# Modulation of a two-layer generator block: from column products on VectorE with sums on TensorE to row products on GpSimd, ScalarE and VectorE

## The chip, the cores and the metric

The kernel runs on one core of a Trainium2 chip, which has five engines with a queue each: TensorE (PE in the profile, PEld its weight loads), VectorE (DVE), ScalarE (ACT), GpSimd (POOL) and SyncE (SP), which issues most DMAs. Each engine takes its queue in order. The metric is the device time of one execution in microseconds (us), as the median of several runs.

## The reference

Two trunk layers over 256 context tokens and 1024 latent tokens, 1024 channels, all in 32-bit floats. What the change touches is the modulation: six vectors of 1024 numbers for each layer and each of two conditioning rows (`c` for the latents, `c_ctx` for the context).

```python
for layer in range(DEPTH):            # 2
    mod_l = (silu(c)     @ w_ada[layer] + b_ada[layer])      # w_ada: (2, 1024, 6144)
    mod_c = (silu(c_ctx) @ w_ada[layer] + b_ada[layer])
    sh1, sc1, g1, sh2, sc2, g2 = split(mod, 6)               # for _l and _c
    p = split_proj((rmsnorm(x) * (1 + sc1) + sh1) @ w_in[layer])
    x = x + g1 * mixer_out(four_scans(p), p, g_heads[layer], w_out[layer])
    x = x + g2 * square(relu((rmsnorm(x) * (1 + sc2) + sh2) @ w_ff1[layer])) @ w_ff2[layer]
return rmsnorm(x) * g_final
```

## The kernel before

Channels lie on the 128 partitions and tokens along the free dimension (NT = 1280 of both kinds). Large products are three matmuls each (`mm3`, lines 291 to 295), since every operand is split into a high and a low half; `whalf` (line 275) loads a weight tile of 128x512, makes its high half on ACT (line 281) and its low half on DVE (line 282).

For each layer `build` runs the norm and the projection of values (`mix_open`), then the four head groups (`mixers`), the output projection (`outproj`) and the channel sub-layer (`mlp`). In `mixers` two streams are interleaved: the scans (`mix_vec`, `mix_ml`, `mix_rt`, much of it on DVE and ACT) and dense projections that fill PE (`Fill`). In `mlp` 16 pairs of hidden tiles follow each other: 6 blocks of 24 matmuls, whose results ACT and DVE square and split (lines 502 to 505), then 24 blocks of 6 matmuls, which DVE adds into the residual (line 525, an "evacuation" below).

The modulation `mod` has 48 columns of 128 for each layer, in three parts r of 16 columns. Part 0 of layer 0 is made ahead on PE (`ada_unit`, `ada_finish`). The other five parts are made beside other work by the generator `ada_part` (line 391). It goes over a group of W columns: for each k of 8 it loads w_ada of 128 input channels by W columns (line 402), multiplies every partition by its conditioning number, and adds to an accumulator A on DVE (line 406 for k = 0, line 408 after), one accumulator for each conditioning row. Then PE sums A over the partitions with a vector of ones, 128 columns at a time (line 413, one output column each), and DVE adds the bias (line 419) and, for the scales, 1 (line 421).

- Parts 1 and 2 of layer 0 run in `mixers` of layer 0: W = 256, four weight buffers, both rows from one load, 128 loads of 128 KB. `Fill.step` takes a step of the generator (one load with its products) at three of five of its own steps (line 175); what is left runs at the end (line 1500).
- The three parts of layer 1 run in `mlp` of layer 0: W = 512, four weight buffers, 96 loads of 256 KB, four steps after each hidden tile (`filler`, line 1611). Parts 1 and 2 need the latents' row alone.

The order of the instructions on each engine is worked out when the program is built, by readiness of operands and buffers, and not by the order of the source alone; at run time it is fixed. All loads named here are issued by SP.

Of the kernel before, what the change touches and what calls it, by code (L numbers as in the profile page):

```python
# [6 lines left out]
F32 = mybir.dt.float32  # L7
# [190 lines left out]
class K:  # L198
    def __init__(self, ctx, tc, io):
# [16 lines left out]
        self.d_a = dp.tile([2, 4, NC], F32, name="d_a")  # L216

# [105 lines left out]

    def params2(self, tmp):
# [66 lines left out]
    def ada_part(self, l, r, toks, wring, tmp, acc, banks, W):  # L391


        nc = self.nc
        one = self.m64[:, 1:2]
        nt, nb = len(toks), W // 128
        for q in range(2048 // W):
            g, h = divmod(q * W, 512)
            A = [b(W) for b in acc[:nt]]
            for k in range(NK):  # L400
                w = wring.next()(W)
                nc.sync.dma_start(w, self.io["w_ada"][l, r, k, :, g, h:h + W])
                for i, j in enumerate(toks):
                    c = self.cc[:, k, j:j + 1]
                    if k == 0:
                        nc.vector.tensor_scalar(A[i], w, c, None, op0=ALU.mult)
                    else:
                        nc.vector.scalar_tensor_tensor(A[i], w, c, A[i], op0=ALU.mult, op1=ALU.add)
                yield
            ps = self.bank(banks().next())  # L410
            for i in range(nt):
                for cb in range(nb):
                    nc.tensor.matmul(ps[:, 2 * cb + i:2 * cb + i + 1], lhsT=A[i][:, 128 * cb:128 * cb + 128], rhs=one,  # L413
                                     start=True, stop=True)
            o = 16 * r + nb * q
            mo = self.mod[:, l, o:o + nb, toks[0]:toks[0] + nt]
            bb = self.bada[:, l, o:o + nb].unsqueeze(2).to_broadcast([128, nb, nt])
            v = ps[:, 0:2 * nb].rearrange("p (c j) -> p c j", j=2)[:, :, 0:nt]
            nc.vector.tensor_tensor(mo, v, bb, op=ALU.add)
            if (r == 0 and g >= 2) or (r == 2 and g < 2):  # L420
                nc.vector.tensor_scalar(mo, mo, 1.0, None, op0=ALU.add)
            yield
# [997 lines left out]
    def mixers(self, l, ada):  # L1420
# [36 lines left out]
        if l == 0:  # L1457
            fill.also = ada([ao.sub(256 * i, 256) for i in range(6)], lambda: self.dbanks)
# [112 lines left out]
def build(ctx, tc, io):  # L1571
# [16 lines left out]
    b.params2(b.tmps.next())  # L1588
    for l in range(2):
# [148 lines left out]
```

## Time and profile before

| | |
|---|---|
| median of 3 runs | 3310.36 us (3309.62 to 3310.97) |
| profiled execution | 3300.05 us |
| its span, first to last instruction | 3298.2 us |
| mean granted TensorE clock | 0.992 |
| busy: PE, PEld, DVE, ACT, POOL | 97%, 80%, 64%, 39%, 0% |
| chain that ended last | PE 88%, DVE 5%, DMA 3%, ACT 3% |
| mixers of layer 0 | about 220 to 770 us |
| channel sub-layer of layer 0 | about 930 to 1840 us |

Busy time is the union of an engine's instructions; matmuls are pipelined, so a busy PE is one that always has one under way. The chain is followed back from the last instruction to what released it at each step. A wait is told by the waiting engine and line, and what released it.

### The profile page before, as it was taken

Reading aid. Unit: us, or ns where it says so; the run is one execution under the profiler, and the core shown is the slowest. Engines: PE = TensorE matmul, PEld = TensorE weight load, DVE = VectorE, ACT = ScalarE, POOL = GpSimd, SP = SyncE. Lnnn points to the kernel's source line nnn. Section 1 sums busy time; section 2 is a strip of 40 time slices with the busy share of each in tenths; the row PEclk is TensorE's granted clock in tenths of the full one; section 3 lists DMA queues with packets and bytes.
Section 4 is the critical chain, followed back from the end, with each engine's and each line's share of the span. In section 5 each row is a group of like instructions: output and inputs, shape, how many; then the busy total and the mean of one; then the engine's idle time right before and its main releaser. Section 6 shows DMA issues by size and latency. Waiting matters only on the chain.

```text
span 3298.2 us, 52930 instructions
## 1 busy us (share of the span) xinstructions
PE 3215.6 (97%) x20936; PEld 2640.0 (80%) x20936; DVE 2121.8 (64%) x4218; ACT 1286.1 (39%) x2665; POOL 10.8 (0%) x41
## 2 busy tenths in 40 slices
PE   7998899999999999999999999999999999999998
PEld 4786688877888888888888678788778888888887
DVE  4778887787666656555655586866756555554546
ACT  4665565445322122121212565765445322222222
POOL 0000000000000000000000000000000000000000
PEclk9999899999999999999999999999999999999999
DMA  5113444434322222222211222333315111111111
GB/s 206 61 50 127 122 133 148 121 101 146 103 80 71 83 65 80 69 64 64 77 39 34 76 66 77 110 114 109 103 58 163 53 50 46 51 51 46 51 48 65
DMA packets 175010, 278.85 MB, mean 85 GB/s; under 512 B 21097, under 2 KB 66825, under 8 KB 174505
## 3 DMA queue, kind: packets, MB, share of 16 engines
q1 hardware_dynamic: 173464, 273.66, 26.5%
q8 instruction: 164, 2.69, 0.3%
q10 hardware_dynamic: 1296, 1.81, 0.2%
q14 instruction: 86, 0.70, 0.1%
HBM read 229.75 MB, written 45.64 MB: 83 GB/s over the span
## 4 chain that ended last, share of the span: by engine, by line
PE 88%; DVE 5%; DMA 3%; ACT 3%; issue 1%; SPq 0%; DVEq 0%; ACTq 0%
PE psum L293 23%; PE psum L294 23%; PE psum L295 23%; PE psum L830 2%; PE psum L600 2%; PE psum L631 2%; PE psum L633 2%; PE psum L632 1%; PE psum L817 1%; PE psum L833 1%; PE psum L1018 1%; PE psum L705 1%; PE psum L1357 1%; PE psum L413 1%; DVE px L990 1%
## 5 line engine op out<-in xcount | busy, mean ns | idle before, releaser
L525 DVE SCALAR_TENSOR_TENSOR x<-psum,st,x 128x512 f32<-128x512 f32 (+1 forms) x648 | 441.3, 690 | 213.2 <-PE psum L295 212.3
L281 ACT ACTIVATE pc<-st 128x512 fp32r<-128x512 f32 x256 | 161.2, 632 | 847.5 <-PE psum L294 808.7
L294 PE MATMUL psum<-pc,pc 128*128 128x512 f32 (+1 forms) x1296 | 475.9, 367 | 0.0
L293 PE MATMUL psum<-pc,pc 128*128 128x512 f32 (+1 forms) x1296 | 475.8, 367 | 0.0
L295 PE MATMUL psum<-pc,pc 128*128 128x512 f32 (+1 forms) x1296 | 473.8, 366 | 0.0
L293 PE MATMUL psum<-Hhi,pc 128*128 128x512 f32 (+1 forms) x1280 | 471.9, 369 | 1.7 <-ACT pc L281 1.5
L294 PE MATMUL psum<-Hlo,pc 128*128 128x512 f32 (+1 forms) x1280 | 471.9, 369 | 0.1
L295 PE MATMUL psum<-Hhi,pc 128*128 128x512 f32 (+1 forms) x1280 | 470.5, 368 | 0.0
L293 PE MATMUL psum<-Hhi,pw 128*128 128x512 f32 (+1 forms) x1192 | 451.0, 379 | 5.7 <-ACT pw L281 2.5
L295 PE MATMUL psum<-Hhi,pw 128*128 128x512 f32 (+1 forms) x1192 | 445.2, 374 | 0.0
L294 PE MATMUL psum<-Hlo,pw 128*128 128x512 f32 (+1 forms) x1192 | 444.8, 373 | 0.0
L504 DVE TENSOR_TENSOR st<-st 128x256 f32<-128x256 f32 (+1 forms) x160 | 101.8, 637 | 301.8 <-ACT pc L503 300.7
L293 PEld LDWEIGHTS psum<-pc,pc 128*128 128x128 f32 x1296 | 244.4, 189 | 43.8 <-DVE x L525 1.3
L295 PEld LDWEIGHTS psum<-pc,pc 128*128 128x128 f32 x1296 | 244.0, 188 | 43.0 <-issue 2.7
L294 PEld LDWEIGHTS psum<-pc,pc 128*128 128x128 f32 x1296 | 244.5, 189 | 41.3 <-issue 2.1
L293 PEld LDWEIGHTS psum<-Hhi,pc 128*128 128x128 f32 x1280 | 241.2, 189 | 43.5 <-ACT pc L281 2.4
L294 PEld LDWEIGHTS psum<-Hlo,pc 128*128 128x128 f32 x1280 | 241.3, 189 | 40.9 <-DVE Hlo L481 0.5
L295 PEld LDWEIGHTS psum<-Hhi,pc 128*128 128x128 f32 x1280 | 241.1, 188 | 40.9 <-DVE pc L282 0.6
L293 PEld LDWEIGHTS psum<-Hhi,pw 128*128 128x128 f32 x1192 | 226.7, 190 | 51.4 <-issue 10.1
L282 DVE TENSOR_TENSOR pc<-st,pc 128x512 fp32r<-128x512 f32 x256 | 175.5, 690 | 137.9 <-ACT pc L281 117.3
L295 PEld LDWEIGHTS psum<-Hhi,pw 128*128 128x128 f32 x1192 | 226.2, 190 | 37.6 <-issue 2.1
L294 PEld LDWEIGHTS psum<-Hlo,pw 128*128 128x128 f32 x1192 | 226.8, 190 | 36.2 <-issue 2.2
(398 smaller groups left out, 4950.4 us busy)
## 6 DMA issues: line engine op xcount, KB each, us to landing
st<-w_ff SPq DMA_DIRECT2D x256, 256.0 KB
st<-w_inT SPq DMA_DIRECT2D x96, 256.0 KB
ph<-w_ada SPq DMA_DIRECT2D x128, 128.0 KB
st<-w_out SPq DMA_DIRECT2D x50, 256.0 KB
pc<-w_ada SPq DMA_DIRECT2D x48, 256.0 KB
st<-w_ada SPq DMA_DIRECT2D x48, 256.0 KB
d_z<-st SPq DMA_DIRECT2D x40, 256.0 KB
ps<-w_ada SPq DMA_DIRECT2D x32, 256.0 KB
```

What stands on the lines that cost most here:

```text
L281: nc.scalar.activation(hi, raw, AF.Copy)
L282: (eng or nc.vector).tensor_tensor(lo, raw, F(hi), op=ALU.subtract)
L293: t.matmul(out, lhsT=w[0], rhs=m[0], start=first, stop=False)
L294: t.matmul(out, lhsT=w[0], rhs=m[1], start=False, stop=False)
L295: t.matmul(out, lhsT=w[1], rhs=m[0], start=False, stop=last)
L413: nc.tensor.matmul(ps[:, 2 * cb + i:2 * cb + i + 1], lhsT=A[i][:, 128 * cb:128 * cb + 128], rhs=one, start=True, stop=True)
L504: nc.vector.tensor_tensor(r, r, r, op=ALU.mult)
L525: nc.vector.scalar_tensor_tensor(x, ps, self.mod[:, l, 40 + o, j:j + 1], x, op0=ALU.mult, op1=ALU.add)
L600: t.matmul(ps[:, 0:304], lhsT=h[a], rhs=u[b], start=(k + i == 0), stop=(k == NK - 1 and i == 2))
L631: t.matmul(ps[:, e, :], lhsT=h[0], rhs=u[0], start=(k == 0), stop=False)
L633: t.matmul(ps[:, e, :], lhsT=h[1], rhs=u[0], start=False, stop=(k == NK - 1))
L830: nc.tensor.matmul(o, lhsT=ST[r0:r0 + kd, c, d, :], rhs=qd[d](c)[r0:r0 + kd, :], start=(j == 0), stop=False, tile_position=(r0, 0))
```

## The change

The loads now hold rows of the transposed weights: 128 output columns on the partitions and 512 of the 1024 input channels along the free dimension (`w_adaR`, laid out on the host). The conditioning row must then lie along the free dimension, the same on each partition: `cond_rows` transposes the 16 conditioning columns on PE once, writes them to DRAM (`d_c`), and `ada_rows` fetches half a row at a time to all partitions. One step multiplies a load by the row and sums it along the free dimension into one column of a scratch, which lies in that part of `mod` that belongs to the other layer. In layer 0's mixers GpSimd multiplies and ScalarE sums, by a copy that also gives out its sum (two weight buffers and one for the row, 256 KB a load, 128 loads, since each conditioning row now has its own loads). In layer 0's `mlp`, for layer 1, one VectorE instruction does both (five weight buffers and one for the row, 128 loads of 256 KB); a step there is two loads, and three steps follow a hidden tile. The two halves are added and the bias and the 1 follow on VectorE. PE has no part in it.

```diff
+    def cond_rows(self, tmp):
...
+        T = self.bank(self.banks.next())[0:16, 0:128]
+        a, b = tmp.sub(0, 16)(16), tmp.sub(16, 128)(128)
+        nc.vector.tensor_copy(a.rearrange("p (j k) -> p k j", k=NK), self.cc[:, :, 0:2])
+        nc.tensor.transpose(T, a, self.ident)
+        nc.vector.tensor_copy(b[0:16], T)
+        nc.gpsimd.dma_start(self.d_c.rearrange("j k p -> (j k) p"), b[0:16])
...
-    def ada_part(self, l, r, toks, wring, tmp, acc, banks, W):
...
+    def ada_rows(self, l, r, toks, wring, cs, queue, several=1):
...
+        S = self.mod[:, 1 - l, 0:16, :]
+        for j in toks:
+            for h in range(2):
+                c = cs.next()(512)
+                queue.dma_start(c.rearrange("p (k q) -> p k q", q=128), self.d_c[j:j + 1, 4 * h:4 * h + 4, :].to_broadcast([128, 4, 128]))
+                for o in range(16):
+                    w = wring.next()(512)
+                    queue.dma_start(w, self.io["w_adaR"][l, r, o, :, 512 * h:512 * h + 512])
+                    if l == 0:
+                        nc.gpsimd.tensor_tensor(w, w, c, op=ALU.mult)
+                        nc.scalar.activation(w, w, AF.Copy, accum_out=S[:, o:o + 1, h])
                     else:
+                        nc.vector.scalar_tensor_tensor(w, w, 1.0, c, op0=ALU.mult, op1=ALU.mult, accum_out=S[:, o:o + 1, h])
+                    if o % several == several - 1:
+                        yield
+            mo = self.mod[:, l, 16 * r:16 * r + 16, j]
+            nc.vector.tensor_tensor(mo, S[:, :, 0], S[:, :, 1], op=ALU.add)
+            nc.vector.tensor_tensor(mo, mo, self.bada[:, l, 16 * r:16 * r + 16], op=ALU.add)
...
-            fill.also = ada([ao.sub(256 * i, 256) for i in range(6)], lambda: self.dbanks)
+            fill.also = ada([ao.sub(512 * i, 512) for i in range(3)])
...
+    b.cond_rows(b.tmps.next())
...
-                yield from b.ada_part(0, r, (0, 1), Ring(bufs[:4]), None, bufs[4:6], banks, 256)
+                yield from b.ada_rows(0, r, (0, 1), Ring(bufs[:2]), Ring(bufs[2:]), nc.sync)
...
-                yield from b.ada_part(1, r, (0, 1) if r == 0 else (1,), Ring(bufs[:4]), None, bufs[4:6], lambda: b.banks, 512)
+                yield from b.ada_rows(1, r, (0, 1) if r == 0 else (1,), Ring(bufs[:5]), Ring(bufs[5:]), nc.sync, 2)
...
-            for _ in range(4):
+            for _ in range(3):
                 next(gen, None)
```

Three places show the order on the engines. The numbers after L are lines of the kernel concerned; the new file's lines are some five further on (its 822 is 817 before, its 504 to 510 are 499 to 505, its 530 is 525).

TensorE in the mixers, second scan of the first kind (817: state products of the scan; 892: transposes; 293 to 295: dense projections; 413: sums of the modulation), before:

```order
L817 MATMUL psum<-ph_0_251,px_0_688 64x64
L294 MATMUL psum<-Hlo,pw_0_247 128x512
L295 MATMUL psum<-Hhi,pw_0_247 128x512
L413 MATMUL psum<-st,ph_0_251 128x1 x2
L817 MATMUL psum<-ph_0_251,px_0_688 64x64 x8
L892 MATMUL psum<-st,px_0_688 128x128 x4
L413 MATMUL psum<-st,ph_0_251 128x1 x2
L293 MATMUL psum<-Hhi,pw_0_247 128x256
```

The sums of the modulation are gone from TensorE's order, 64 rows of them in each stage (the trace records each as two passes).

ScalarE in the mixers, same scan, its third group of chunks (305 to 309 and 653: gate functions of projections; 937, 953, 989, 993: exponentials of the scan; 282: high half of a weight; 416: the new sum), now:

```order
L416 ACTIVATE ph_0_256,st<-ph_0_256 128x512
L993 ACTIVATE px_0_693<-px_0_693 128x512
L989 ACTIVATE px_0_693<-px_0_693 128x512
L416 ACTIVATE ph_0_256,st<-ph_0_256 128x512
L653 ACTIVATE st<-st 128x512
L282 ACTIVATE pw_0_252<-st 128x512
L416 ACTIVATE ph_0_256,st<-ph_0_256 128x512
L282 ACTIVATE pw_0_252<-st 128x512
L305 ACTIVATE st<-psum 128x512
L953 ACTIVATE px_0_693<-px_0_693 128x512
L416 ACTIVATE ph_0_256,st<-ph_0_256 128x512
```

A sum now stands after every two or three of ScalarE's own instructions; before, no instruction of the modulation was on this queue.

VectorE in the channel sub-layer, end of a pair's hidden tiles (504 and 505: square and low half of the activations; 282: low half of a weight; 406, 408: products; 419: bias), before:

```order
L505 TENSOR_TENSOR pc_9_8783<-st,pc_8_8782 128x512
L282 TENSOR_TENSOR pc_0_8774<-st,pc_0_8774 128x512
L406 TENSOR_SCALAR st<-pc_4_8778,st 128x512
L419 TENSOR_TENSOR st<-psum,st 128x8
L406 TENSOR_SCALAR st<-pc_4_8778,st 128x512
L408 SCALAR_TENSOR_TENSOR st<-pc_5_8779,st 128x512
L504 TENSOR_TENSOR st<-st 128x512
L408 SCALAR_TENSOR_TENSOR st<-pc_5_8779,st 128x512
L505 TENSOR_TENSOR pc_9_8783<-st,pc_8_8782 128x512
```

And now, at the end of the second pair's hidden tiles (418: product with its sum; 509 and 510 are 504 and 505 before; 283 is 282):

```order
L418 SCALAR_TENSOR_TENSOR st<-st 128x512
L510 TENSOR_TENSOR pc_11_8724<-st,pc_10_8723 128x512
L418 SCALAR_TENSOR_TENSOR pc_4_8717,st<-pc_4_8717,st 128x512
L509 TENSOR_TENSOR st<-st 128x256
L418 SCALAR_TENSOR_TENSOR pc_5_8718,st<-pc_5_8718,st 128x512
L510 TENSOR_TENSOR pc_7_8720<-st,pc_6_8719 128x256
L418 SCALAR_TENSOR_TENSOR st<-st 128x512 x3
L418 SCALAR_TENSOR_TENSOR pc_4_8717,st<-pc_4_8717,st 128x512
L418 SCALAR_TENSOR_TENSOR pc_5_8718,st<-pc_5_8718,st 128x512
L418 SCALAR_TENSOR_TENSOR st<-st 128x512
L509 TENSOR_TENSOR st<-st 128x512
```

The 128 products of layer 1's modulation lay beside 288 of the stage's 384 evacuations; now they lie beside the first 72.

## Rows read from the trace of the kernel before

**Rows 1.** The page: busy us, share and count by engine; the chain's shares.

```profile
PE 3215.6 (97%) x20936; PEld 2640.0 (80%) x20936; DVE 2121.8 (64%) x4218; ACT 1286.1 (39%) x2665; POOL 10.8 (0%) x41
...
PE 88%; DVE 5%; DMA 3%; ACT 3%; issue 1%; SPq 0%; DVEq 0%; ACTq 0%
```

**Rows 2.** Busy us (instructions) by stretch: mixers and channel stage of layer 0.

```profile
core 0: us, PE busy (x) PEld busy (x) DVE busy (x) ACT busy (x) POOL busy (x), PEclk, DMA share, GB/s
220.00:770.00 550.00, 521.27 (x4618) 423.80 (x4614) 449.80 (x1157) 292.39 (x703) 1.53 (x14) 0.97 0.39 118
930.00:1840.00 910.00, 908.93 (x4761) 776.42 (x4760) 538.20 (x889) 204.49 (x364) 0.00 (x0) 1.00 0.23 68
```

**Rows 3.** Line 413's matmuls: count, ns min/median/max, first and last start us.

```profile
L413 PE MATMUL psum<-st,ph x128: 164/250/353, 292.9 to 763.1; 128*128 128x1 f32 x128
...
L413 PE MATMUL psum<-st x128: 164/250/250, 1005.2 to 1682.3; 128*128 128x1 f32 x128
```

**Rows 4.** The chain in order of time: start us, us, what; both stages.

```profile
574.44 0.79 PE psum L413 x8
...
1005.37 1.68 PE psum L413 x16
```

**Rows 5.** PE's waits, 220 to 770 us: releaser, us in total, times, longest.

```profile
PE psum L1018 <- DVE px L990: 10.1, 5, 4.6
...
PE psum L413 <- DVE ph L408: 3.5, 1, 3.5
```

**Rows 6.** DVE by line and shape, 220 to 770 us: busy us, mean ns | idle before.

```profile
L408 DVE SCALAR_TENSOR_TENSOR ph<-ph,st 128x256 f32<-128x256 f32 x224 | 99.7, 479 | 0.2 <-DMA ph<-w_ada 0.2
...
L406 DVE TENSOR_SCALAR ph<-ph,st 128x256 f32<-128x256 f32 x32 | 10.7, 347 | 4.2 <-PE psum L413 4.2
```

**Rows 7.** The same view, 930 to 1840 us.

```profile
L408 DVE SCALAR_TENSOR_TENSOR st<-st 128x512 f32<-128x512 f32 x64 | 46.8, 747 | 3.0 <-DMA st<-w_ada 2.9
...
L408 DVE SCALAR_TENSOR_TENSOR st<-pc,st 128x512 f32<-128x512 f32 x48 | 35.0, 747 | 0.9 <-DMA pc<-w_ada 0.8
...
L406 DVE TENSOR_SCALAR st<-pc,st 128x512 f32<-128x512 f32 x16 | 7.7, 480 | 9.5 <-PE psum L413 9.5
```

**Rows 8.** Busy us by stretch of 40 us (columns as in rows 2).

```profile
300.00:340.00 40.00, 28.52 (x303) 22.78 (x302) 36.01 (x82) 21.68 (x42) 0.00 (x0) 0.83 0.24 80
340.00:380.00 40.00, 34.59 (x344) 27.74 (x342) 34.14 (x75) 23.07 (x45) 0.00 (x0) 0.91 0.34 106
380.00:420.00 40.00, 34.85 (x262) 27.04 (x263) 33.90 (x96) 21.40 (x50) 0.21 (x2) 0.87 0.54 162
sum 120.00, PE 97.96 PEld 77.56 DVE 104.05 ACT 66.15 POOL 0.21; mean PE 32.65 PEld 25.85 DVE 34.68 ACT 22.05 POOL 0.07
```

**Rows 9.** The same three stretches, line 408 alone, then line 406 alone.

```profile
sum 120.00, DVE 23.41; mean DVE 7.80
...
sum 120.00, DVE 1.92; mean DVE 0.64
```

**Rows 10.** Lines 484 and 591 (as rows 3); line 525 at 1845.1 to 1851.5 us.

```profile
L484 POOL TENSOR_TENSOR Hlo<-st,Hhi x5: 1269/1298/1509, 1845.2 to 1855.8; 128x512 fp32r<-128x512 f32 x5
...
L591 DVE TENSOR_TENSOR pw<-st,pw x16: 464/474/1553, 34.7 to 1857.3; 128x304 fp32r<-128x304 f32 x16
...
L525 DVE SCALAR_TENSOR_TENSOR x<-psum,st,x 128x512 f32<-128x512 f32 x4 | 2.7, 741 | 0.0
```

**Rows 11.** ACT: a copy of 128x512 (as rows 6); the smallest ACTIVATE (as rows 3).

```profile
L281 ACT ACTIVATE pc<-st 128x512 fp32r<-128x512 f32 x128 | 80.6, 632 | 471.1 <-PE psum L294 438.9 <-DMA pc<-w_ada 24.6 <-PE psum L295 4.0
...
L867 ACT ACTIVATE ph<-ph x12: 193/208/214, 102.5 to 2188.8; 128x10 f32<-128x10 f32 x12
```

**Rows 12.** The chain in order of time: DMAs of 192 and 256 KB.

```profile
577.73 4.32 DMA ph<-d_u
...
796.46 3.42 DMA st<-w_out
...
803.48 4.64 DMA st<-w_out
```

**Rows 13.** SP: issue of line 402's loads (as rows 3); SP's longest wait, 220 to 770 us.

```profile
L402 SPq DMA_DIRECT2D ph<-w_ada x128: 327/332/1240, 223.7 to 743.6; - x128
...
SPq L402 <- DVE ph L408: 77.3, 63, 9.6
```

**Rows 14.** Busy us by stretch, channel stage, without modulation (columns as in rows 2).

```profile
1690.00:1747.00 57.00, 57.00 (x298) 48.97 (x297) 27.66 (x44) 12.08 (x22) 0.00 (x0) 1.00 0.12 37
1747.00:1804.00 57.00, 57.00 (x297) 48.98 (x296) 28.85 (x46) 11.89 (x22) 0.00 (x0) 1.00 0.11 34
```

**Rows 15.** DVE: first products of the channel stage, and the smallest instruction (as rows 3).

```profile
L406 DVE TENSOR_SCALAR st<-pc,st x16: 477/479/486, 937.1 to 1626.5; 128x512 f32<-128x512 f32 x16
...
L421 DVE TENSOR_SCALAR st<-st x8: 163/166/168, 534.0 to 1570.7; 128x4 f32<-128x4 f32 x6, 128x8 f32<-128x8 f32 x2
```

**Rows 16.** DVE's timeline: start us, us, what; three like instructions back to back.

```profile
1838.59 2.08 DVE L476 SCALAR_TENSOR_TENSOR st<-x,st 128x512 f32<-128x512 f32 x3 [0.32 <-ACT st L454]
```

More of the change, by code (lines that the diff above doesn't have):

```diff
@@ L216, in __init__ @@
         self.d_a = dp.tile([2, 4, NC], F32, name="d_a")
+        self.d_c = dp.tile([2, 8, 128], F32, name="d_c")
     @staticmethod
@@ L322, in params @@
         nc.vector.tensor_tensor(c2, c2, b, op=ALU.mult)
+    def cond_rows(self, tmp):
+        nc = self.nc
+        T = self.bank(self.banks.next())[0:16, 0:128]
[4 more added lines that the diff above has]
+        nc.gpsimd.dma_start(self.d_c.rearrange("j k p -> (j k) p"), b[0:16])
     def params2(self, tmp):
@@ L389, in ada_finish @@
             nc.vector.tensor_scalar(m, m, 1.0, None, op0=ALU.add)
-    def ada_part(self, l, r, toks, wring, tmp, acc, banks, W):
+    def ada_rows(self, l, r, toks, wring, cs, queue, several=1):
         nc = self.nc
[L395 to L406, printed above, removed]
-                    else:
[L408 to L420, printed above, removed]
@@ new lines, in ada_rows @@
+        S = self.mod[:, 1 - l, 0:16, :]
[9 more added lines that the diff above has]
+                        nc.scalar.activation(w, w, AF.Copy, accum_out=S[:, o:o + 1, h])
+                    else:
+                        nc.vector.scalar_tensor_tensor(w, w, 1.0, c, op0=ALU.mult, op1=ALU.mult, accum_out=S[:, o:o + 1, h])
[4 more added lines that the diff above has]
+            nc.vector.tensor_tensor(mo, mo, self.bada[:, l, 16 * r:16 * r + 16], op=ALU.add)
+            if r in (0, 2):
+                mo = self.mod[:, l, 16 * r + (8 if r == 0 else 0):16 * r + (16 if r == 0 else 8), j]
@@ L1592, in build, with ada @@
         b.mix_open(l)
-        def ada(bufs, banks):
+        def ada(bufs):
             for r in (1, 2):
-                yield from b.ada_part(0, r, (0, 1), Ring(bufs[:4]), None, bufs[4:6], banks, 256)
+                yield from b.ada_rows(0, r, (0, 1), Ring(bufs[:2]), Ring(bufs[2:]), nc.sync)
         b.mixers(l, ada)
@@ L1707, in host @@
     A["gla_w"] = ga
-    A["w_ada"] = ca(w_ada.reshape(2, 8, 128, 3, 4, 512).transpose(0, 3, 1, 2, 4, 5))
+    A["w_ada"] = ca(w_ada[:1, :, :2048].reshape(1, 8, 128, 1, 4, 512).transpose(0, 3, 1, 2, 4, 5))
+    A["w_adaR"] = ca(w_ada.transpose(0, 2, 1).reshape(2, 3, 16, 128, 1024))
     at = _cols()
```

## The prediction

> **What bounds the kernel now.** I read the page first: busy time by engine, then the chain that ended last [rows 1]. TensorE is busy 3215.6 of 3298.2 us and the chain is 88% PE, with 5% DVE, 3% ACT and 3% DMA. So what is taken from TensorE comes off the time, and what another engine gains counts only where TensorE waits for it. The table by stretches [rows 2] then tells the two stages that the change touches apart. In the mixers of the first layer (220 to 770 us) PE is busy 521.3 of 550 us, DVE 449.8, ACT 292.4. In the first layer's channel stage (930 to 1840 us) PE is busy 908.9 of 910 us, so nothing is waited for, while DVE has 538.2 of 910 us. The next view is the same table at 40 us [rows 8]: of the 29 us that PE is idle in the mixers, 22 lie between 300 and 420 us, where DVE is busy 104 of 120 us and the granted clock is 0.83 to 0.91, that is, some of the time the lower level (1.2 GHz). There DVE is the bound; in the rest of the mixers it is PE.
>
> **What it removes from TensorE.** The old scheme ends each group of columns with sums over partitions on PE (line 413): 256 recorded matmuls, 128 in each stage [rows 3]. The chain prices them: 16 in a row take 1.68 us, 8 in a row 0.79 us [rows 4]. Channel stage: 128/16 x 1.68 = 13.4 us; mixers: 128/8 x 0.79 = 12.6 us. In the one wait that PE had for such a sum's operand, it idled 3.5 us [rows 5]. All of this stood on PE's own queue with PE busy before and behind it, so I count it in full: 13.4 + 12.6 + 3.5 = 29.5 us off. The one transpose that is added (16 columns, once, early) is at the price of a short matmul, under 0.5 us by the 0.25 us median of line 413's: nothing.
>
> **What it moves in the mixers.** The products of line 408 (224 at 0.479 us) and line 406 (32 at 0.347 us) leave DVE, 110.4 us of its 449.8 [rows 6]. In their place come 128 products of 128x512 on GpSimd and 128 copies with a sum on ScalarE. Three prices follow.
>
> First, GpSimd's product. The only like row is the subtraction of line 484, 128x512 with two SBUF inputs: 1.30 us [rows 10]. 128 of them are 166 us of an idle engine, so the product itself is hidden. What it does to DVE is not. In the 4 us in which three such GpSimd instructions ran, line 591 on DVE, which also reads two SBUF tensors, took up to 1.553 us where its median is 0.474, while line 525, which reads one from PSUM, kept 0.741 us on average [rows 10]. So one GpSimd product costs DVE from 0 (nothing with two SBUF inputs waits then) to 1.08 us. Over 128 that is 0 to 138 us, against the 110 us that DVE is rid of. Where DVE is idle a fifth of the time this costs little; between 300 and 420 us it decides. There lines 408 and 406 have 23.4 + 1.9 us [rows 9], and by the order of the changed kernel, matched to the times of before, 39 products lie there: 0 to 42 us, and I take 0.8 us each, 31 us, since DVE is busy 87% of that stretch and most of its work reads two SBUF tensors. Net +6 us, between -10 (DVE's relief gives back half of PE's idle 22 us) and +17.
>
> The Trainium skill has a rule for this: "SBUF — State Buffer", section "Who interferes with whom", says that a VectorE instruction with two SBUF inputs and a GpSimd instruction that reads SBUF exclude each other for a whole instruction, whichever comes second waiting. The trace agrees (1.553 for 0.474 us). Held strictly, each product would cost nearly its whole length and the relief of VectorE would be void; that is the second rival below.
>
> Second, ScalarE's sum. A copy of 128x512 from SBUF takes 0.63 us, and the smallest ACTIVATE 0.21 us [rows 11], so a copy that also hands out its sum costs 0.63 to 0.84 us: 81 to 108 us more on ACT, on top of 292 of 550. That alone is no bound. But ACT takes its queue in order, and behind each sum stand evacuations of PSUM and exponentials that PE and DVE wait for. The sum waits for GpSimd's product, this for its load, and the load for the sum two steps before, since there are two weight buffers where before there were four. One round of a buffer is: issue 0.33 us [rows 13], landing of 256 KB 3.42 to 4.64 us with some other traffic [rows 12], product 1.30, sum 0.63 to 0.84: 5.7 to 7.1 us, so with two buffers a step each 2.8 to 3.6 us. In the order, the dense stretches hold 43 steps beside what took 139 us before (294 to 433 us) and 40 beside 119 us (448 to 567 us): 258/83 = 3.1 us a step. So the round is about as long as the work beside it. I take 3.2 us, 83 x 0.1 = +8 us; the ends are 0 (at 2.8) and 83 x 0.5 = +41 us (at 3.6). Each of the eight changes of the conditioning row costs a broadcast load more; the nearest row is the broadcast of d_u, 4.32 us [rows 12], and it is hidden where ACT has other work, which is in the 8.
>
> SP's queue gets these loads too: one waits for a ScalarE sum, and behind it stand the fetches of other weights. Before, they waited for DVE in the same place, 77.3 us in 63 times [rows 13]. The bytes double to 33.5 MB in a stage that moves 118 GB/s [rows 2]; spread over 550 us that is 30 GB/s more, and I take it as hidden.
>
> **What it moves in the channel stage.** 112 products at 0.747 and 16 at 0.480 us [rows 7], 91 us of DVE, become 128 with a sum: 0.69 us each back to back (three like instructions took 2.08 us [rows 16]), plus 0 to 0.16 us if the sum is handed out by a small instruction of its own (0.166 us is the price of the smallest [rows 15]). The new thing is where they stand. The old chain hung on PE's sums and PSUM banks, which spread it from 937 to 1682 us [rows 3, 15]. The new one hangs on nothing but its loads, and the order puts all 128 beside the first 72 of 384 evacuations, what lies between 936 and 1126 us before. Per 57 us (the stretch in which PE does one pair of hidden tiles) this is 38 products: DVE's own work is 28.3 us [rows 14], so 28.3 + 38 x 0.69 = 54.5 us without and 60.6 us with a separate hand-out, against 57.0 - 1.7 = 55.3 us of PE. DVE is full for 3.3 such pairs, and comes out between nothing and 5.3 x 3.3 = 18 us late. I take +5 us, near the low end, since back-to-back spacing leaves room and PE has eight PSUM banks to run ahead in. What is late next if the cover goes is the low half of the weights (line 282) and of the activations (line 505), which PE reads at once.
>
> **The sum.** -29.5 + 6 + 8 + 5 = -10.5 us. The profiled execution took 3300.05 us (span 3298.2); the median of the runs is 3310.36, 10.3 us more. 3300.05 - 10.5 = 3289.6, and as a median 3299.9 us.
>
> **Rivals.** (a) More comes back. DVE's relief wins between 300 and 420 us, and neither ACT nor DVE is late elsewhere: -29.5 - 10 = -39.5, 3271 us. For it: PE idles there behind DVE's line 990 [rows 5] and the clock is low [rows 8]. Against it: the 1.553 us of line 591 [rows 10].
>
> (b) DVE is no freer than before. Every GpSimd product costs DVE the 1.08 us that line 591 lost [rows 10]: +17 us between 300 and 420 us, and the channel stage is 8 us late: -29.5 + 17 + 8 + 8 (the round) = +3.5, some 3314 us, within no change. For it: the row of line 591; against it: DVE has room in the mixers outside 300 to 420 us [rows 2, 8]. It is what the rule of the Trainium skill's "SBUF — State Buffer" gives when every product finds such an instruction beside it.
>
> (c) Slower: ScalarE is held. In the mixers ACT stands before the sums with PE's evacuations behind them. It decides from the point at which a round of a buffer is longer than what stands beside two steps, 6.2 us; a landing of 4.64 us and a product that waits half a microsecond for DVE are enough. Price +41 us for the dense stretches at 3.6 us a step, with the other terms as taken: -29.5 + 6 + 41 + 5 = +22.5, 3333 us. For it: two buffers, and an order fixed ahead of the run. Against it: before, DVE waited only 0.2 us for the same loads in this stage [rows 6], with 128 KB and four buffers.
>
> **How the numbers follow.** Forecast (a gain of 7 to 25 us, 3285 to 3303) 0.41; (a) 0.07; (b), within 6.6 us of now, 0.22; (c) 0.30. A change under 0.2% (6.6 us) is about what a measurement of this kernel can't tell from none. Faster 0.48, same 0.22, slower 0.30. The range leaves out the far part of (a) and of (c): 3280 to 3336 us.
>
> **What would show it.** Right: no matmul of one column in the trace; channel stage shorter by some 8 us, DVE busy over 0.9 between about 936 and 1130 us and under 0.55 after it; ACT's waits for GpSimd small, under 30 us in all; DVE's two-input instructions with maxima over 1.5 us in the mixers. Wrong: ACT waits for GpSimd of 50 us and more and mixers longer than 550 us (c); PE idle in the channel stage by over 15 us, which would make my +5 the failing term; or 300 to 420 us as short as PE's work, which would be (a).

## The result, and the profile after

The changed kernel takes 3345.7 us (median of 4 runs, 3336.37 to 3351.86); before, on the same chip, 3309.99 us (4 runs, 3305.33 to 3310.97). The ratio is 1.0108, 95% interval 1.0077 to 1.014: 36 us slower, where 10 us faster was forecast, and outside the range. The profiled execution took 3336.37 us, 36.3 us more than that of before. Of all runs told here one, of e1_mlp_alone, took 5210 us at a granted clock of 0.554; it is left out of that kernel's ratio.

Lines of the new file are some five further on than those of before: 990 is now 995, 1018 is 1023, 505 is 510, 281 and 282 are 282 and 283. New are 410 and 413 (loads of the row and of the weights), 415 (GpSimd's product), 416 (ScalarE's sum) and 418 (VectorE's product with its sum).

First the page of the changed kernel, busy us by engine and the chain's shares, to be held against [rows 1]:

```profile
PE 3211.5 (96%) x20681; PEld 2626.1 (79%) x20681; DVE 2112.6 (63%) x4077; ACT 1363.8 (41%) x2921; POOL 188.8 (6%) x170
...
PE 77%; DVE 10%; DMA 6%; ACT 4%; issue 1%; POOL 1%; SPq 0%; DVEq 0%; ACTq 0%; POOLq 0%
```

TensorE and VectorE have slightly less to do than before, and still the end is later: the chain has lost 11 points of PE to DVE and DMA.

Where the time went is told by milestones that both kernels have. From the first matmul of line 955 to the first addition of line 1564 (in the numbers of before) the mixers' part lasted 647.0 us and lasts 37.1 more. From the first square of line 504 to the last addition of line 525 the channel stage lasted 898.4 us and lasts 3.2 less. What lies between, before and after adds +2.5 us in all. Within the mixers, a square on ScalarE (line 702) that stood at 287 us before comes 7 us later, the one at 424 us 25 later, at 481 us 34, at 553 us 44, at 611 us 51; after that 14 us come back.

Two stretches between the same instructions, before (287 to 424 us, and on to the end of the part) and then after (294 to 449 us, and on; columns as in rows 2):

```profile
287.00:424.00 137.00, 114.51 (x1049) 90.59 (x1047) 118.64 (x291) 80.18 (x177) 0.32 (x3) 0.89 0.38 119
424.00:826.00 402.00, 395.97 (x3159) 327.37 (x3156) 317.29 (x792) 208.48 (x501) 1.21 (x11) 1.00 0.42 128
```

```profile
294.00:449.00 155.00, 132.12 (x1131) 104.36 (x1131) 120.12 (x215) 106.96 (x265) 60.76 (x49) 0.90 0.50 160
449.00:865.00 416.00, 382.12 (x2938) 310.45 (x2938) 303.46 (x603) 249.83 (x644) 104.12 (x83) 0.96 0.44 140
```

In the first stretch TensorE idles 23 us, as it did before; it is 18 us longer because TensorE has 18 us more to do there, as the new order puts more projections into it. The loss lies in the second: TensorE idled 6.0 of 402 us and now idles 33.9 of 416, with a granted clock of 0.96, that is, part of the time at the lower level (1.2 GHz). VectorE is busy only 303 of these 416 us, 73%.

What TensorE waits for: its largest wait in 220 to 800 us is the third line here; the two above it are waits of the new scheme's own queues (releaser, us in total, times, longest):

```profile
POOL ph L415 <- DMA ph<-w_adaR: 296.9, 98, 25.5
...
ACT ph L416 <- POOL ph L415: 57.1, 58, 2.9
PE psum L1023 <- DVE px L995: 29.7, 20, 4.9
```

In [rows 5] the same wait for line 990 was 10.1 us in 5 times. Its instruction, before and then after (ns min/median/max, first and last start us):

```profile
L990 DVE SCALAR_TENSOR_TENSOR px<-px,st x100: 474/747/755, 288.0 to 2268.1; 128x512 f32<-128x512 f32 x80, 128x256 f32<-128x256 f32 x20
```

```profile
L995 DVE SCALAR_TENSOR_TENSOR px<-px,st x100: 472/751/1793, 290.8 to 2303.8; 128x512 f32<-128x512 f32 x80, 128x256 f32<-128x256 f32 x20
```

It took 0.755 us at most and takes up to 1.793 us now. By shape in the mixers (220 to 800 us; busy us, mean ns | idle before), with one of line 311 beside it that reads PSUM and one SBUF tensor:

```profile
L995 DVE SCALAR_TENSOR_TENSOR px<-px,st 128x512 f32<-128x512 f32 x40 | 39.1, 976 | 4.1 <-ACT px L993 3.4
...
L995 DVE SCALAR_TENSOR_TENSOR px<-px,st 128x256 f32<-128x256 f32 x20 | 17.2, 861 | 2.2 <-ACT px L993 1.4
...
L311 DVE SCALAR_TENSOR_TENSOR st<-psum,st 128x512 f32<-128x512 f32 x16 | 10.9, 681 | 0.7 <-ACT st L309 0.7
```

The form of two SBUF inputs has a mean of 0.976 us instead of 0.747, line 311 keeps its 0.68 us. Comparing every VectorE instruction of the mixers with the median of its line and shape before, 99 of them are over 0.3 us longer (none by more than 1.14 us) and all together they take 86.6 us more: 0.68 us for each of the 128 products on average. ScalarE's instructions of the same stretch, compared in the same way, are no longer than before. One such place in the timeline, GpSimd, then VectorE, then TensorE (start us, us, what, idle before and its releaser):

```profile
398.14 1.41 POOL L415 TENSOR_TENSOR ph<-ph 128x512 f32<-128x512 f32 x1 [0.88 <-DMA ph<-w_adaR]
401.36 1.27 POOL L415 TENSOR_TENSOR ph<-ph 128x512 f32<-128x512 f32 x1 [1.81 <-DMA ph<-w_adaR]
```

```profile
398.36 1.48 DVE L981 TENSOR_TENSOR px<-px 128x256 f32<-128x256 f32 x1
...
400.60 2.58 DVE L995 SCALAR_TENSOR_TENSOR px<-px,st 128x512 f32<-128x512 f32 x2
```

```profile
397.98 0.28 PE L294 MATMUL psum<-Hhi,pw 128*128 128x256 f32 x1
398.10 0.28 PE L295 MATMUL psum<-Hlo,pw 128*128 128x256 f32 x1
403.32 1.08 PE L1023 MATMUL psum<-px 128*32 128x64 f32 x32 [4.95 <-DVE px L995]
...
404.71 0.41 PE L294 MATMUL psum<-Hhi,pw 128*128 128x256 f32 x1
404.93 0.41 PE L295 MATMUL psum<-Hlo,pw 128*128 128x256 f32 x1
```

The two instructions of line 995 take 2.58 us, for two times 0.75; the first stands alone and the second, with a product beside it, takes 1.79. TensorE idles 4.95 us, and behind that its matmuls of 128x256 follow each other at 0.22 us where they did at 0.12: the clock has fallen to the lower level. Summed over the mixers, the records of the granted clock hold 30.7 us at the lower level before and 64.8 after.

In the channel stage the single product costs what was expected (684 ns and 81 ns for its sum):

```profile
L418 DVE SCALAR_TENSOR_TENSOR st<-st x74: 676/684/693, 996.7 to 1178.6; 128x512 f32<-128x512 f32 x74
L418 DVE DVE_READ_ACCUMULATOR st<-st x74: 77/81/86, 997.3 to 1179.2; 128x1 f32 x74
```

TensorE there has one wait of 6.8 us, where before none was over 0.8, and VectorE stands for the conditioning row (waits, 940 to 1250 us):

```profile
DVE pc L418 <- DMA st<-d_c: 11.5, 5, 4.0
DVE st L418 <- DMA st<-d_c: 6.9, 2, 3.8
PE psum L295 <- DVE pc L510: 6.8, 1, 6.8
```

### The profile page after: what moved, and what is told of

Its sections match the earlier page's. It is cut to its first block, busy times and chain, and to the rows that moved or that the text cites. A ratio compares the mean times of both kernels' runs of the same rounds, so it can differ in the third digit from the quotient of the medians.

```text
span 3334.6 us, 52712 instructions
## 1 busy us (share of the span) xinstructions
PE 3211.5 (96%) x20681; PEld 2626.1 (79%) x20681; DVE 2112.6 (63%) x4077; ACT 1363.8 (41%) x2921; POOL 188.8 (6%) x170
## 4 chain that ended last, share of the span: by engine, by line
PE 77%; DVE 10%; DMA 6%; ACT 4%; issue 1%; POOL 1%; SPq 0%; DVEq 0%; ACTq 0%; POOLq 0%
PE psum L294 20%; PE psum L296 20%; PE psum L295 20%; PE psum L835 2%; PE psum L605 2%; DVE px L995 1%; DMA ph<-w_adaR 1%; PE psum L838 1%; PE psum L636 1%; PE psum L638 1%; PE psum L637 1%; PE psum L822 1%; PE psum L1362 1%; PE psum L1023 1%; PE psum L710 1%
## 5 line engine op out<-in xcount | busy, mean ns | idle before, releaser
L294 PE MATMUL psum<-Hhi,pw 128*128 128x512 f32 (+1 forms) x1192 | 456.7, 383 | 5.3 <-ACT pw L282 4.6
L296 PE MATMUL psum<-Hhi,pw 128*128 128x512 f32 (+1 forms) x1192 | 451.3, 379 | 0.6 <-DVE pw L283 0.5
L294 PEld LDWEIGHTS psum<-Hhi,pw 128*128 128x128 f32 x1192 | 230.4, 193 | 53.1 <-issue 10.9
L296 PEld LDWEIGHTS psum<-Hhi,pw 128*128 128x128 f32 x1192 | 230.3, 193 | 40.6 <-issue 2.7
L295 PEld LDWEIGHTS psum<-Hlo,pw 128*128 128x128 f32 x1192 | 230.7, 194 | 37.1 <-issue 2.5
```

The lines of the kernel that those rows point to most:

```text
L294: t.matmul(out, lhsT=w[0], rhs=m[0], start=first, stop=False)
L295: t.matmul(out, lhsT=w[0], rhs=m[1], start=False, stop=False)
L296: t.matmul(out, lhsT=w[1], rhs=m[0], start=False, stop=last)
```

## Experiments

Two theories for the mixers. **G**: GpSimd's product holds up VectorE's instructions with two SBUF inputs, and TensorE waits behind those. **S**: ScalarE, in order, stands at its sums for the round of product and load, and what is queued behind comes late (rival (c)). For the channel stage: **F**, VectorE is full of products (the prediction's term), against **R**, its queue stands for the row, and **W**, for the weights.

All runs in one table: change of the mixers' part and of the channel stage against before (by the milestones above, one execution each), how much longer VectorE's instructions of the mixers took in all, and the time at the lower clock in the mixers. Ratios are to runs of before beside them.

| kernel | median us (runs) | ratio, 95% | mixers | channel | VectorE longer | lower clock |
|---|---|---|---|---|---|---|
| changed kernel | 3345.7 (4) | 1.0077 to 1.014 | +37.1 | -3.2 | 86.6 | 64.8 |
| e1_mlp_alone | 3300.32 (10) | 0.9965 to 0.9994 | +4.1 | -5.7 | 0 | 44.4 |
| e2_gpsimd_only | 3328.8 (1) | | +33.3 | -3.2 | 91.3 | 41.0 |
| e3_scalar_only | 3263.08 (1) | | -34.0 | -5.6 | 0.4 | 0 |
| e4_mix_vector | 3281.7 (4) | 0.9902 to 0.9943 | -20.9 | -6.4 | 0 | 30.7 |
| e5_vector_two_rows | 3284.81 (4) | 0.9911 to 0.995 | -16.0 | -3.7 | 0 | 34.1 |
| e6_vector_three_loads | 3276.26 (4) | 0.9891 to 0.9924 | -18.1 | -5.6 | 0 | 20.5 |
| e7_gpsimd_writes | 3273.53 (1) | | -22.7 | -4.7 | 0.4 | 17.1 |
| e8_gpsimd_one_input | 3303.09 (1) | | +1.0 | -6.5 | 22.3 | 30.7 |
| e9_one_row_load | 3272.89 (1) | | -23.8 | -12.5 | 1.7 | 17.1 |
| e10_no_loads | 3268.53 (1) | | -26.2 | -14.6 | 1.4 | 17.1 |
| e11_rows_kept | 3280.52 (6) | 0.9893 to 0.993 | -24.1 | -7.3 | 0 | 23.9 |

How fine this is: e6, e9, e10 and e11 have the same mixers and differ by 8 us there; e1 has the mixers of before and +4.1. Between the last addition of the first channel stage and the first of the second, where nine of the twelve kernels of the table (all but the changed one, e2 and e8) have the same order on VectorE and ScalarE, these nine took from 756 to 770 us. So differences of the mixers under some 15 us are not told apart by one execution each. The channel stage has the same source in the changed kernel, in e1 to e4 and in e6 to e8, with -3.2 to -6.5: there, differences under some 4 us are not told apart.

Two rivals run through all of these. The order of the engines in the mixers is made anew for each kernel, and VectorE's differs between the changed kernel, e2, e3, e4, e6, e7 and e8; but the two with some 90 us of longer instructions are 33 and 37 us slower, all without are 16 us or more faster (e1, with the mixers of before, aside), and the one with 22 us lies between. And the doubled bytes, which the prediction took as hidden, are loaded in e3 to e11 as well.

**e1_mlp_alone**: the mixers as before, the channel stage as changed.

```diff
...
-                yield from b.ada_rows(0, r, (0, 1), Ring(bufs[:2]), Ring(bufs[2:]), nc.sync)
+                yield from b.ada_part(0, r, (0, 1), Ring(bufs[:4]), None, bufs[4:6], banks, 256)
...
```

> The mixers make their modulation as before the change (columns on VectorE, sums on TensorE); only the channel stage has the new row products on VectorE. In the changed kernel's profile the channel stage came out about 3 us shorter and the mixers about 43 us longer than before. If the loss lies in the mixers alone, this kernel takes 3300 to 3310 us (no loss, a gain of up to 10), and from the first square of the channel stage on (line 504 before) it is 2 to 13 us shorter than before. If the channel stage only looked short because the mixers had shifted it, it takes 3320 us or more.

Measured: 7 us faster than before, the channel stage 5.7 us shorter. Both are as the first case has them: the loss lies in the mixers' half of the change, and the other half brings less than TensorE's 13.4 us.

**e2_gpsimd_only**: the product without ScalarE's sum.

```diff
+        if l == 0:
+            nc.vector.memset(S, 0.0)
...
                         nc.gpsimd.tensor_tensor(w, w, c, op=ALU.mult)
-                        nc.scalar.activation(w, w, AF.Copy, accum_out=S[:, o:o + 1, h])
```

> Changed kernel without ScalarE's sums in the mixers (the sums are left out, so layer 0's modulation is wrong; GpSimd multiplies as in the change, and a load waits for GpSimd alone). Theory G (GpSimd's products hold up VectorE's instructions that read two SBUF tensors): VectorE's instructions are stretched by 60 to 90 us in all as in the changed kernel (87 us), and the mixers stay 25 us or more longer than before the change. Theory S (ScalarE stands before its sums, 57 us in the changed kernel, with TensorE's work behind it): the stretching may stay, but the mixers come out at most 10 us longer than before, or shorter.

Measured: the loss stays, +33.3 us, as theory G has it. VectorE's line (996 here) is as much longer:

```profile
L996 DVE SCALAR_TENSOR_TENSOR px<-px,st x100: 473/751/1870, 291.8 to 2296.4; 128x512 f32<-128x512 f32 x80, 128x256 f32<-128x256 f32 x20
...
PE psum L1024 <- DVE px L996: 27.6, 24, 2.7
```

Nothing of ScalarE hangs on GpSimd here, so S isn't needed for the loss: the 4 us between this kernel and the changed one are not told from nothing.

**e3_scalar_only**: the sum without the product.

```diff
-                        nc.gpsimd.tensor_tensor(w, w, c, op=ALU.mult)
                         nc.scalar.activation(w, w, AF.Copy, accum_out=S[:, o:o + 1, h])
```

> Changed kernel without GpSimd's products in the mixers (ScalarE sums the loads themselves; the conditioning row is left out, so layer 0's modulation is wrong). Theory G: no VectorE instruction is stretched, and the mixers are 5 to 20 us shorter than before the change. Theory S: ScalarE still stands before its sums, now for the loads, 30 us or more, and the mixers stay 20 us or more longer than before.

Measured: the mixers are 34.0 us shorter than before, 71 shorter than in the changed kernel, with line 995 (994 here) at its old length and ScalarE standing 30 us for the loads:

```profile
L994 DVE SCALAR_TENSOR_TENSOR px<-px,st x100: 483/750/754, 289.2 to 2230.4; 128x512 f32<-128x512 f32 x80, 128x256 f32<-128x256 f32 x20
...
ACT ph L415 <- DMA ph<-w_adaR: 30.4, 39, 1.8
```

This is the direction that G gives, 14 us beyond its range. With e2 it points to G; that the product's reads do it, and not the longer round through GpSimd, is left to e7. In the 34 us lies the gain that the forecast saw: TensorE's sums in the mixers (12.6 + 3.5 us by the rows of before; no run takes them away alone) and the lower clock, which fell from 30.7 us to none.

**e4_mix_vector**: VectorE multiplies and sums in the mixers too, as in the channel stage.

```diff
-                        nc.gpsimd.tensor_tensor(w, w, c, op=ALU.mult)
-                        nc.scalar.activation(w, w, AF.Copy, accum_out=S[:, o:o + 1, h])
+                        nc.vector.scalar_tensor_tensor(w, w, 1.0, c, op0=ALU.mult, op1=ALU.mult, accum_out=S[:, o:o + 1, h])
```

> Changed kernel whose row products in the mixers are made and summed by one VectorE instruction as in the channel stage: neither GpSimd nor ScalarE takes part. 128 instructions of 0.684 and 0.081 us are 98 us of VectorE against 110 us before the change, without stretching. Both theories expect most of the loss gone: 3290 to 3310 us. If it stays at 3325 us or more, neither the exclusion nor ScalarE's queue is the cause but what both share: two buffers for the loads, so that whichever engine multiplies stands in its queue for the next load.

Measured: 3281.7 us, faster than both kernels and than the expected 3290 to 3310. VectorE's products take 98 us, little less than the 110 that the old scheme had there [rows 6], and do no harm that can be told here:

```profile
L415 DVE SCALAR_TENSOR_TENSOR ph<-ph 128x512 f32<-128x512 f32 x128 | 87.2, 686 | 17.8 <-DMA ph<-w_adaR 14.4 <-DMA ph<-d_c 3.1
...
L415 DVE DVE_READ_ACCUMULATOR ph<-ph 128x1 f32 x128 | 10.6, 83 | 0.0
```

98 us of VectorE in its own queue cost less than 87 us that GpSimd takes from it. A likely reason, not tested by itself, is that the order on the engines was made with the first in it and without the second.

**e5_vector_two_rows** and **e6_vector_three_loads**: from e4, two row buffers and four weight buffers in the channel stage; and three weight buffers instead of two in the mixers.

```diff
-                yield from b.ada_rows(1, r, (0, 1) if r == 0 else (1,), Ring(bufs[:5]), Ring(bufs[5:]), nc.sync, 2)
+                yield from b.ada_rows(1, r, (0, 1) if r == 0 else (1,), Ring(bufs[:4]), Ring(bufs[4:]), nc.sync, 2)
```

> The kernel with row products on VectorE in both stages (3281.7 us), and in the channel stage two buffers for the conditioning row and four for the loads instead of one and five. If what the channel stage gives back (7 of the 13.4 us of TensorE's sums; VectorE stands 12 us for the row's loads) comes from the change of the row, VectorE's waits for d_c fall under 4 us and the stage gets 4 to 7 us shorter: 3274 to 3278 us. If VectorE is simply full while it makes the products, nothing changes: 3280 to 3284 us.

```diff
-        ao = hp.alloc(1536, True) if l == 0 else None
+        ao = hp.alloc(2048, True) if l == 0 else None
...
-            fill.also = ada([ao.sub(512 * i, 512) for i in range(3)])
+            fill.also = ada([ao.sub(512 * i, 512) for i in range(4)])
...
-                yield from b.ada_rows(0, r, (0, 1), Ring(bufs[:2]), Ring(bufs[2:]), nc.sync)
+                yield from b.ada_rows(0, r, (0, 1), Ring(bufs[:3]), Ring(bufs[3:]), nc.sync)
```

> The kernel with row products on VectorE in both stages, and in the mixers three buffers for the loads instead of two. If two buffers still cost (VectorE stood 14.4 us for these loads, 24 times), the mixers get 3 to 15 us shorter and the kernel takes 3265 to 3279 us. If the waits were beside the path, it stays within 5 us of 3281.7 us; the order of all engines changes with the buffers, so the mixers may also move some us either way.

Measured: in e5 VectorE's standing for the row is gone, and it stands for weights instead; TensorE's wait stays and the time is 3284.81 us. The first case missed, and the second has the time but not the reason (waits of e5):

```profile
DVE pc L417 <- DMA pc<-w_adaR: 11.5, 13, 2.1
PE psum L295 <- DVE pc L509: 7.3, 2, 6.0
```

e6 is the fastest whole kernel, 3276.26 us, inside the first case's 3265 to 3279, but the mixers are not shorter than in e4 (-18.1 to -20.9) and its interval overlaps that of e4: the third buffer isn't shown to count.

**e7_gpsimd_writes** and **e8_gpsimd_one_input**: what of GpSimd's work holds VectorE. In e7 two fills that read nothing stand in place of the product, in e8 a multiplication by 1.0 that reads one tensor.

```diff
-                        nc.gpsimd.tensor_tensor(w, w, c, op=ALU.mult)
+                        for _ in range(2):
+                            nc.gpsimd.memset(w, 1.0)
```

> The changed kernel with two memsets of the load's buffer on GpSimd in place of the product (the product is left out, so layer 0's modulation is wrong); ScalarE sums as in the change, and all waits are as there. GpSimd is then about as busy (128x256 takes 0.31 us, so some 1.1 us a step against 1.3) but reads nothing from SBUF. If GpSimd's reading is what stops VectorE's instructions with two SBUF inputs, none is stretched and the mixers come out 20 to 35 us shorter than before the change, as without GpSimd. If any work of GpSimd does it, by its writes or by the chain load, GpSimd, ScalarE, the stretching is 50 us or more and the mixers are longer than before.

```diff
-                        nc.gpsimd.tensor_tensor(w, w, c, op=ALU.mult)
+                        nc.gpsimd.tensor_scalar(w, w, 1.0, None, op0=ALU.mult)
```

> The changed kernel with a GpSimd instruction that reads one SBUF tensor (times 1.0) in place of the product (the conditioning row is left out, so layer 0's modulation is wrong). If one read is enough to hold VectorE for the instruction's whole time, the stretching per step is as long as this instruction is against the product: 87 us times its duration over 1.39 us, and the mixers stand between before and the change in the same measure. If it takes two reads, there is no stretching and the mixers are 20 us or more shorter than before.

Measured, e7: GpSimd is busy 134.7 us with writes alone, VectorE's line (996 here) keeps its length, and the mixers are 22.7 us shorter than before although ScalarE stands 48.6 us for GpSimd, nearly the changed kernel's 57.1. The first case holds:

```profile
L996 DVE SCALAR_TENSOR_TENSOR px<-px,st x100: 477/750/755, 289.2 to 2240.4; 128x512 f32<-128x512 f32 x80, 128x256 f32<-128x256 f32 x20
...
ACT ph L417 <- POOL ph L416: 48.6, 42, 5.0
```

So the link through GpSimd is worth some 11 us (-34.0 to -22.7), not told from nothing, and the other 60 or so of GpSimd's 71 us come with its reads. e8 falls between its two cases: held for the whole instruction, VectorE would be 94 us longer (87 x 1.494/1.39). One read lengthens VectorE by 22.3 us, 19.3 of them in 48 instructions, none by more than 0.46 us, and the mixers come out as before (+1.0):

```profile
L415 POOL TENSOR_SCALAR ph<-ph x128: 1482/1494/2353, 232.4 to 715.2; 128x512 f32<-128x512 f32 x128
...
L995 DVE SCALAR_TENSOR_TENSOR px<-px,st x100: 471/752/1186, 294.4 to 2263.5; 128x512 f32<-128x512 f32 x80, 128x256 f32<-128x256 f32 x20
```

The Trainium skill ("SBUF — State Buffer", section "Who interferes with whom") says that a VectorE instruction with two SBUF inputs contends with a GpSimd instruction that reads SBUF, not with one that only writes, and that one with at most one SBUF input, outside VectorE's 2-port modes, doesn't. e7, line 311 and line 995 agree. That the one that comes second stands for a whole instruction, as the prediction took from the page, nearly agrees for the two-input product (up to 1.14 us longer beside products of 1.30) and not for the one-input one: up to 0.46 us, and on average 0.17 us a product (22.3/128) beside 0.68, though it is longer (1.494 us).

**e9_one_row_load** and **e10_no_loads**: from e6, the channel stage with one row load instead of eight; and then with one weight load too, which all products read.

```diff
+        c = getattr(self, 'row', None)
...
-                c = cs.next()(512)
-                queue.dma_start(c.rearrange("p (k q) -> p k q", q=128), self.d_c[j:j + 1, 4 * h:4 * h + 4, :].to_broadcast([128, 4, 128]))
+                c = cs.next()(512) if l == 0 or (r, j, h) == (0, 0, 0) else c
+                if l == 0 or (r, j, h) == (0, 0, 0):
+                    queue.dma_start(c.rearrange("p (k q) -> p k q", q=128), self.d_c[j:j + 1, 4 * h:4 * h + 4, :].to_broadcast([128, 4, 128]))
+                self.row = c
...
```

> e6_vector_three_loads, but in the channel stage the conditioning row is loaded once only, and seven of its eight loads are left out (layer 1's modulation is then made with the wrong row). All weight loads, all products and their sums stay. Theory R (VectorE's queue stands for the row, 18 us in 7 times, and PE's evacuations behind it come late): the 6 us wait of PE for line 510's result (another number here) and the low clock behind it go, channel stage 9 to 13 us shorter than before instead of 5.6. Theory W (the weight loads come too late as well; two row buffers only moved the wait to them): VectorE waits 8 to 15 us for weight loads, PE's wait stays at 4 to 7 us, channel stage 4 to 7 us shorter. Theory F (VectorE is full of products): as W in PE's wait, but VectorE waits under 5 us for loads.

```diff
-                    queue.dma_start(w, self.io["w_adaR"][l, r, o, :, 512 * h:512 * h + 512])
+                    if l == 0:
+                        queue.dma_start(w, self.io["w_adaR"][l, r, o, :, 512 * h:512 * h + 512])
+                    elif (r, j, h, o) == (0, 0, 0, 0):
+                        queue.dma_start(kept, self.io["w_adaR"][l, r, o, :, 512 * h:512 * h + 512])
...
-                        nc.vector.scalar_tensor_tensor(w, w, 1.0, c, op0=ALU.mult, op1=ALU.mult, accum_out=S[:, o:o + 1, h])
+                        nc.vector.scalar_tensor_tensor(w, kept, 1.0, c, op0=ALU.mult, op1=ALU.mult, accum_out=S[:, o:o + 1, h])
...
```

> As e9_one_row_load, and the channel stage's weight loads are left out too: one weight tile is loaded once, and all 128 products there read it and write to the other four buffers, so layer 1's modulation is not the reference's. Nothing of the products can then wait for a load. Theories R and W: PE's wait of 6 us for VectorE's low half is gone, the low clock with it, and the channel stage is 10 to 14 us shorter than before, as the 13.4 us of TensorE's sums say. Theory F (products at 0.77 us each beside VectorE's own work fill it): the products stand closer together, PE's wait stays at 5 us or more, channel stage under 7 us shorter.

Measured: e9's channel stage is 12.5 us shorter than before, TensorE's wait 1.6 us, none of it at the lower clock; e10's is 14.6 us shorter with no such wait (2.1 us more, not told from nothing). The stretch of the products in e10 (columns as in rows 2):

```profile
920.00:980.00 60.00, 60.00 (x309) 51.16 (x308) 59.29 (x138) 17.30 (x32) 0.00 (x0) 1.00 0.11 36
980.00:1040.00 60.00, 60.00 (x312) 51.48 (x311) 59.83 (x157) 12.82 (x23) 0.00 (x0) 1.00 0.11 37
```

VectorE is busy 59.3 and 59.8 of 60 us and TensorE loses nothing: F is refuted. The 13.4 us of TensorE's sums are there in full, and the row's loads took most of them back: R.

**e11_rows_kept**: the whole result with four row loads instead of eight; two row buffers keep the latents' halves, four weight buffers.

```diff
-                c = cs.next()(512)
-                queue.dma_start(c.rearrange("p (k q) -> p k q", q=128), self.d_c[j:j + 1, 4 * h:4 * h + 4, :].to_broadcast([128, 4, 128]))
+                c = held.get((j, h))
+                if c is None:
+                    c = held[j, h] = cs.next()(512)
+                    queue.dma_start(c.rearrange("p (k q) -> p k q", q=128), self.d_c[j:j + 1, 4 * h:4 * h + 4, :].to_broadcast([128, 4, 128]))
...
```

> e6_vector_three_loads with the whole result and four row loads instead of eight in the channel stage: two row buffers and four weight buffers, and the latents' two half rows stay for layer 1's second and third part. If VectorE's standing for the row is what delays PE there (theory R, after e9_one_row_load), PE's wait of 6 us goes or falls under 3 us, the channel stage is 9 to 13 us shorter than before instead of 5.6, and the median is 3267 to 3274 us against 3276 of e6_vector_three_loads. If the fourth weight buffer less makes the weight loads late instead (as e5_vector_two_rows had it, where all eight rows were loaded), VectorE waits some 10 us for weights, PE's wait stays at 4 to 7 us and the time at that of e6_vector_three_loads, 3274 to 3282 us.

Measured: 3280.52 us, the second of the two cases: with a weight buffer less, VectorE stands for weights and TensorE's wait stays (waits, 920 to 1250 us).

```profile
DVE pc L420 <- DMA pc<-w_adaR: 8.8, 8, 1.7
DVE st L420 <- DMA st<-w_adaR: 8.5, 10, 2.1
PE psum L295 <- DVE pc L512: 5.3, 2, 3.6
```

So with five weight buffers the row's loads are what costs (R, shown by e9); with four, the waits of e5 and e11 point to the weights (W), which no run took away by themselves. Within six buffers one gives way to the other. Whether one row buffer with four loads and five weight buffers would keep e9's gain wasn't tried.

## Why the prediction was wrong, point by point

**The step that failed: "Net +6 us", GpSimd's hold on VectorE, charged to 39 products.** The price of one was right (0 to 1.08 us, 0.8 taken; 0.68 on average), and so was the row it came from [rows 10]. What failed is the sentence behind it, that where VectorE is idle a fifth of the time this costs little. The products cost VectorE 86.6 us over the whole part. In the stretch that the sum charged (287 to 424 us before) TensorE's idle time and its time at the lower clock stayed as they were, 23 and 31 us; behind it, where the sum had nothing, TensorE's idle time went from 6 to 34 us and its time at the lower clock from 0 to 31. A busy share doesn't tell whether an instruction is waited for. What left VectorE (lines 406 and 408) had cost TensorE little: one wait of 3.5 us, for a sum's operand [rows 5], and 98 us of products put back on VectorE (e4) make the mixers 13 us longer than in e3, not told from nothing. Of the 99 instructions that got longer, 47 are steps of the scan, lines 980 to 995, and TensorE's wait for line 995 tripled (10.1 to 29.7 us), while VectorE's busy time in this part even fell, from 513.6 to 506.8 us.

**The clock** had no term of its own. With the new waits came 34 us more at the lower level in the mixers. At half the rate that is up to 17 us, beside 33 us more of idle TensorE (28.7 of 550 us in [rows 2], 61.9 of 580 now) and 12.6 us of removed sums: 33 + 17 - 12.6 = 37, which is the measured 37.1. This is an estimate: for e2 (62.5 us idle, 10 us more at the lower clock) the same sum gives 26, with 33.3 measured. The prediction read the low clock in [rows 8] as a sign, not as something that another engine's delay would extend.

**TensorE's sums, -29.5 us**: borne out in the channel stage, 13.4 us (14.6 in e10). In the mixers the 16.1 us fit in e3's 34.0, which hold the clock and VectorE's relief too, and are not measured alone. That is rival (a)'s mechanism, which exists once GpSimd doesn't multiply.

**The round of a load, +8 us**: not contradicted, 11 us by e7 against e3 and 4 by e2, neither told from nothing. The signs of rival (c) came true, 57.1 us of ScalarE waiting and 37 us more of mixers, and its time, 3333, was the nearest to 3345.7. Its mechanism was not the cause, so that nearness is luck. Even the chain of waits seems to speak for it (start us, us, what):

```profile
306.96 2.56 DMA ph<-w_adaR
309.58 2.24 POOL ph L415
312.60 2.68 DMA ph<-w_adaR
315.35 1.83 POOL ph L415
```

It runs over the round, but with the sum taken away (e2) the mixers are about as long, and with the round kept and the product's reads taken away (e7) they are 60 us shorter than in the changed kernel. In e3, with mixers 34 us shorter than before, these loads still have a third of the chain between 300 and 420 us. A chain names one of several paths of like length. And the product in it is itself stretched, 2.24 us for 1.30: the two engines hold each other.

**Rival (b)** had the right mechanism, "no freer than before", and failed by the same step: 17 us for 300 to 420 us alone, where TensorE lost nothing more, and nothing for the rest.

**The channel stage, -8.4 us**: -3.2 and, alone (e1), -5.7. The +5 for a full VectorE was the wrong reason for a loss of about the right size: VectorE at 99% costs nothing (e10). One wait of 6.8 us and the lower clock behind it (10.2 us) came from the row's loads, which the prediction put under "hidden", in the mixers, and left out here. The sign named for it, PE idle by over 15 us, was not reached: TensorE idled 7.6 us from 930 to 1840 us, where [rows 2] has 1.1. Nor was VectorE busy over 0.9 there: it was 0.86 between 990 and 1180 us.

## What to carry to other kernels

Before an idle engine gets work, ask what it shares with a busy one, and charge the price to every instruction that is moved, not only where the busy engine is full: a longer step on the way to the bound engine's next matmul can cost its length, and a stretch at the lower clock behind it, also where the engine that makes the step is idle a quarter of the time. Work that nobody waits for is cheap where it is; here leaving the products on VectorE, in one instruction with its sum, was 0.8% faster than the kernel before (e4). To tell which of two paths is the cause, take each away in turn; a long wait (57 us of ScalarE) and the chain both pointed to the wrong one.

## What had not been expected of the hardware

- GpSimd's instruction that only writes costs VectorE nothing (0.4 us in 134.7 us of it, e7); with one SBUF input 0.17 us each on average (e8), with two 0.68 us (changed kernel) and 0.71 us (e2). The most that one VectorE instruction took longer was 0.46 us with one input and 1.15 us with two, for short and long ones alike.
- The one-input multiplication on GpSimd takes longer than the two-input product, 1.494 us (e8) against 1.297 us (changed kernel) for 128x512, both medians.
- Handing out a sum is a small instruction of its own, 0.187 us on ScalarE and 0.081 us on VectorE, and VectorE's product with it takes 0.684 us, less than the 0.747 us of the same shape with a column of numbers as its scalar [rows 7].
